# Longer leads for the steps behind GpSimd and for the steps that refill a stored weight buffer

## The chip, the cores and the metric

The kernel runs on one core of one Trainium2 chip. The metric is the device time of one execution in microseconds: the median of three runs before the change is 2082.1 us (2080.51 to 2083.09). Matrix products run on TensorE (PE in the profile), elementwise work on VectorE (DVE), ScalarE (ACT) and GpSimd (POOL), and all DMAs are issued by SyncE (SP).

## The reference

A hybrid decoder layer over 2048 tokens of width 1024. It applies an RMSNorm, one combined projection `h @ w_in`, eight heads of a gated delta rule, eight channel groups of a short gated convolution, an output projection with the residual, and a last RMSNorm:

```python
proj = rmsnorm(x, norm_in_w) @ w_in          # q,k,v | z | beta,g | B,C,h,z of the convolutions
qkv  = silu(causal_conv4(qkv));  q, k = l2norm(q) * 128**-0.5, l2norm(k)
o    = gated_delta_rule(q, k, v, g, beta)    # triangular solve per chunk, state carried over chunks
o    = rmsnorm(o, gdn_norm_w) * silu(z)
y    = B * (causal_conv3(C * h) + conv_b) * silu(z_c)
out  = rmsnorm(x + concat(o, y) @ w_out, final_norm_w)
```

## The kernel before, in words

**Tiling.** The tokens are worked in two halves of 1024. The columns of `w_in` are taken in 32 pairs of 128 columns: `kq`, `vz` (a head's key and query, value and gate) and `ca`, `cb` (the convolutions). A pair of one half is one call of `quad`: a seven-product scheme (Strassen's kind) over 512-token blocks, each product 12 matmuls of 128x512 in fp16 (high and low parts), so 84 matmuls a quad, into the banks `ps_d`. A quad takes two of six large buffers `t4` for its results (three where a `vacc` is wanted), and the convolutions hand these back.

**Weights.** In the first half every pair's weights are made on the chip. `fetcher` loads two raw tiles (`raw`, four buffers, so two pairs). `scales` squares them on ScalarE (`junk_sq`), sums them over partitions with one small matmul (`ps_t<-wss,ones_b`) and calls `pow2_below` (line 504) for a power-of-two scale: a maximum on VectorE, a power on GpSimd (`p<-p,nhalf_pow`), a mask on VectorE (`p<-p,expo`), a product. `prepare_hi` (line 735) makes the five high parts on ScalarE, in the order G1, G2, G7, G3, G4. `prepare_lo` (line 749) makes the low parts on VectorE and the sums and differences `st` that they need; one sum, `raw<-raw`, goes to GpSimd or VectorE, whichever is free earlier (`either`). Each of the five buffers exists once: it is written again when its products of the pair before are done and its copy has been stored to DRAM (`keep`, `wc<-g`). The second half reads these copies back (`gr<-wc`) and makes no weights.

**Heads.** For each head `gdn` (line 1102) loads decays (`E`), masks them on GpSimd (`affine_select`), takes eight exponentials on ScalarE, forms `NA` from key products, has `invert` run 31 pairs of small GpSimd steps (`nbt`, `nbx`), and then steps through eight chunks: matmul, `r` on VectorE, matmul, `u` on ScalarE, matmul, the state `S_all` on VectorE.

**Order.** Each engine works its own queue strictly in the order written. That order is made by a planner in the kernel: a `Clock` with costs for each operation advances a time for each engine, generators are the tasks, and `do` (line 340) holds a step back until the planner's time lets it in:

```python
lead = LEAD[e] if lead is None else lead      # 0.0 for ACT, DVE and POOL
t = clk.ready(e, a, k)                        # inputs written, buffer free, by the planner's clock
cur, q = now(), clk.t[e]                      # planner's PE time, the engine's own queue time
late = t > (cur if lead < 0 else max(cur, q)) + lead
if not late and q <= cur + back: break        # then the step is written
```

With lead 0 a step may be written as soon as its inputs are ready by the time that the engine's own queue reaches it; `back` is 1.2. With a negative lead it is written only when the planner's PE time is that much past the moment of readiness. What other tasks write meanwhile goes in front. Some steps have negative leads already: the squares in `scales` (`SAFE`, -5.0) and some steps of the heads (`LATE`, -5.0; -3.0). `keep_order` then fixes each engine's order. The output projection follows at the end, with its own splitting (`split_mix`, which calls `pow2_below` 16 times).

All operations are written by one helper, so every row of the profile has its line, L204; tiles tell them apart.

Of the kernel before, what the change touches and what calls it, by code (L numbers as in the profile page):

```python
# [14 lines left out]
AF = mybir.ActivationFunctionType  # L15
ALU = mybir.AluOpType
# [8 lines left out]
PLAN = ((3, 2, 2, 2, 2, 2, 2, 1), (2, 1, 2, 1, 2, 1, 2, 0))  # L25
SAFE = -5.0
LATE = -5.0
LEAD = {"PE": -0.4, "ACT": 0.0, "DVE": 0.0, "POOL": 0.0, "SP": -2.0}
ORDER = ("PE", "ACT", "DVE", "POOL", "SP")

# [198 lines left out]
def hybrid_layer_kernel(ctx, tc, x, norm_in_w, w_in, conv_qkv_w, A_log, dt_bias, gdn_norm_w,  # L229
# [3 lines left out]
    PE, ACT, DVE, POOL, SP = (Engine(clk, r, k) for r, k in zip(  # L233
        (nc.tensor, nc.scalar, nc.vector, nc.gpsimd, nc.sync), ORDER))
# [52 lines left out]
    def now():  # L287
        return clk.t["PE"]

    def spawn(gen, prio=2):  # L290
        seq[0] += 1
        tasks.append([prio, seq[0], 0.0, gen])
        tasks.sort(key=lambda t: (t[0], t[1]))

    def mark(*key):
        done.add(key)
        marks[0] += 1
# [35 lines left out]
    def need(*keys):  # L333
        while not all(k in done for k in keys):
            yield None
# [4 lines left out]
    def do(fn, *a, back=BACK, lead=None, **k):  # L340
        e = fn.eng
        lead = LEAD[e] if lead is None else lead
        while True:
            t = clk.ready(e, a, k)
            cur, q = now(), clk.t[e]
            late = t > (cur if lead < 0 else max(cur, q)) + lead
            if not late and q <= cur + back:
                break
            yield max(t - max(lead, 0.0) if late else 0.0, q - back, cur + 0.1)
        fn(*a, **k)  # L350
# [21 lines left out]
    def rel(x, n=1):  # L372
        if isinstance(x, str):
            cred[x] += n
        else:
            name = x.tensor.name
            kind, tag = where.pop(name)
            where[tag] = clk.last.get(name, 0.0)
            slots[kind].append(tag)
        marks[0] += 1  # L380
# [13 lines left out]
    def either(n=512):  # L394
        return POOL if max(now(), clk.t["POOL"]) + 0.2 + 0.0026 * n <= \
            max(now(), clk.t["DVE"]) + 1.0 + 0.001 * n else DVE
# [107 lines left out]
    def pow2_below(o, sq, gain):  # L504
        n = sq.shape[-1]
        r = sm.tile([P, 2], F32, tag="p2", name="p2")[:, 0:n]
        yield from do(DVE.tensor_scalar, r, sq, 1e-30, None, op0=ALU.max)
        yield from do(POOL.tensor_tensor, r, r, nhalf_pow[:, 0:n], op=ALU.pow)
        yield from do(DVE.tensor_tensor, r.bitcast(I32), r.bitcast(I32), expo[:, 0:n].bitcast(I32),
                      op=ALU.bitwise_and)  # L510
        yield from do(DVE.tensor_scalar, o, r, gain, None, op0=ALU.mult)

    cols_x = const([P, KD], "cols_x")
# [10 lines left out]
    def scale_x():  # L524
        m = sm.tile([P, KD], F32, tag="m8", name="m8", bufs=1)
        yield from do(DVE.tensor_tensor, m, cols_b[:, 0:KD], cols_b[:, 0:KD], op=ALU.mult)
        m1 = sm.tile([P, 1], F32, tag="m1", name="m1", bufs=1)
        yield from do(DVE.tensor_reduce, m1, m, axis=AX.X, op=ALU.max)
        pt = yield from acq("t")
        yield from do(PE.transpose, pt[0:1, 0:P], m1, ident)  # L530
        m2 = sm.tile([1, 1], F32, tag="m2", name="m2", bufs=1)
        yield from do(DVE.tensor_reduce, m2, pt[0:1, 0:P], axis=AX.X, op=ALU.max)
        yield from do(PE.matmul, pt[:, P:P + 1], ones[0:1, :], m2, start=True, stop=True)
        yield from pow2_below(sx, pt[:, P:P + 1], 256.0)
        rel(pt)
        yield from do(DVE.reciprocal, isx, sx)
        yield from do(DVE.tensor_scalar, cols_x, cols_b[:, 0:KD], sx, None, op0=ALU.mult)
# [168 lines left out]
    def hold(kind):  # L706
        while cred[kind] == 0:
            yield None
        cred[kind] -= 1
# [21 lines left out]
    def parts_of(p):  # L731
        r1, r2 = raws[p, 0], raws[p, 1]
        return r1[:, 0:KT], r1[:, KT:KD], r2[:, 0:KT], r2[:, KT:KD]

    def prepare_hi():
        for p in range(NP):
            yield from need(("s", p))
            s1, s2 = wsc[:, p, 0:1], wsc[:, p, 1:2]
            for tag, dep, nk in (("G1", "s", KD), ("G2", "st", KT), ("G7", "st", KT), ("G3", "st", KD), ("G4", "a12", KT)):
                yield from need((dep, p))  # L740
                yield from hold(tag)
                g = wst.tile([P, 2, nk, P], F16, tag=tag, name="g", bufs=1)
                src = {"G1": lambda: raws[p, 0], "G2": lambda: held[p][:, 0], "G7": lambda: held[p][:, 1],
                       "G3": lambda: raws[p, 1], "G4": lambda: parts_of(p)[1]}[tag]()
                yield from do(ACT.activation, g[:, 0], src, AF.Copy, scale=s2 if tag == "G3" else s1)
                held[p, tag] = g, src
                mark("h", p, tag)

    def prepare_lo():
        def keep(g, at, p):  # L750
            n = 1
            for d in g.shape[1:]:
                n *= d
            yield from do(SP.dma_start, wcd[p][:, at * WG:at * WG + n], g.rearrange("p s k c -> p (s k c)"))

        def low(p, tag, js, at):
            yield from need(("h", p, tag))
            g, src = held.pop((p, tag))
            s = wsc[:, p, 1:2] if tag == "G3" else wsc[:, p, 0:1]
            yield from do(DVE.scalar_tensor_tensor, g[:, 1], src, s, g[:, 0], op0=ALU.mult, op1=ALU.subtract)  # L760
            for o, j in enumerate(js):
                ops[p, j] = lambda k, s, o=o: g[:, s, o * KT + k, :]
                mark("w", p, j)
            spawn(keep(g, at, p), 2)

        for p in range(NP):
            yield from need(("s", p))
            rho = wsc[:, p, 4:5]
            A11, A12, A21, A22 = parts_of(p)
            st = wst.tile([P, 2, KT, P], F32, tag="st", name="st")  # L770
            held[p] = st
            yield from low(p, "G1", (0, 1), 0)
            yield from do(DVE.scalar_tensor_tensor, st[:, 1], A21, rho, A11, op0=ALU.mult, op1=ALU.subtract)
            yield from do(either().tensor_tensor, A21, A21, A22, op=ALU.add)
            yield from do(DVE.scalar_tensor_tensor, st[:, 0], A21, rho, A11, op0=ALU.mult, op1=ALU.subtract)
            mark("st", p)
            yield from do(either().tensor_tensor, A12, A12, st[:, 0], op=ALU.subtract)
            mark("a12", p)
            yield from low(p, "G2", (2,), 2)
            yield from low(p, "G7", (3,), 3)  # L780
            yield from low(p, "G3", (4, 5), 4)
            rel("raw")
            yield from low(p, "G4", (6,), 6)
            rel("raw")
            del raws[p, 0], raws[p, 1], held[p]
        mark("prepared")
# [315 lines left out]
    def gdn(half, h, st):  # L1102
# [6 lines left out]
        beta, dec, ngc, gd = gts[half]  # L1109
        E = hd.tile([P, NC, P], F32, tag="E", name="E", bufs=2)  # L1110
# [1 line left out]
        yield from do(POOL.affine_select, out=E, in_=E, pattern=[[0, NC], [1, P]], compare_op=ALU.is_ge,  # L1112
                      fill=-1e30, base=0, channel_multiplier=-1)
        for c in range(NC):
            yield from do(ACT.activation, E[:, c, :], E[:, c, :], AF.Exp, bias=ngc[:, h, c:c + 1])
        yield from need(("kqt", half, h, 0))
        kqs = st["kq"]
        kss = sm.tile([P, NC], F32, tag="kss", name="kss")
# [24 lines left out]
        for b in range(2):  # L1143
# [8 lines left out]
            for i in range(CB):  # L1152
                c = b * CB + i
# [10 lines left out]
            for c0 in range(b * CB, b * CB + CB, 2):  # L1164
                pq = yield from acq("t")
                for i in range(2):
                    c = c0 + i
# [29 lines left out]
        for b in range(2):  # L1197
            yield from do(DVE.tensor_tensor, kqs[b][:, :, 1, :], qe[:, b * CB:(b + 1) * CB], kqs[b][:, :, 1, :],
                          op=ALU.mult, lead=LATE)

# [5 lines left out]
        for b in range(2):  # L1206
            sl = slice(b * CB, (b + 1) * CB)
            pv = yield from acq("t")
            for i in range(CB):
                c = b * CB + i  # L1210
# [8 lines left out]
        for a, q0 in ((0, 0), (2, 0), (1, 32)):  # L1219
            r0 = a * 32  # L1220
            yield from do(DVE.transpose, V[r0:r0 + 32, :, q0:q0 + 32], W[r0:r0 + 32, :, r0:r0 + 32],
                          lead=-3.0)
# [41 lines left out]
        for b in range(2):  # L1264
            po = yield from acq("o")
            po = po.rearrange("p (c i) -> p c i", i=P)
            for i in range(CB):
                c = b * CB + i
# [6 lines left out]
                else:  # L1275
                    yield from do(PE.matmul, pa, kq(c)[:, 0, :], S, start=True, stop=True)
                    yield from do(DVE.scalar_tensor_tensor, r, pa, dec[:, 0, h, c:c + 1], vp[:, c, :],
                                  op0=ALU.mult, op1=ALU.subtract, back=9.0)
# [7 lines left out]
                else:  # L1286
                    yield from do(DVE.scalar_tensor_tensor, S, S, dec[:, 2, h, c:c + 1], pe,
                                  op0=ALU.mult, op1=ALU.add, back=9.0)
# [5 lines left out]
    def gdn_post(half, h, b, po, qss):  # L1294
# [14 lines left out]
        yield from do(ACT.activation, osq, ocv, AF.Square)  # L1309
        yield from do(DVE.transpose, on, osq, lead=LATE)  # L1310
        op = sm.tile([P, nq], F32, tag="op", name="op")
# [12 lines left out]
        yield from do(DVE.tensor_tensor, ocv, ocv, osq, op=ALU.mult)  # L1324
        yield from do(DVE.scalar_tensor_tensor, zb, oc, gnw, zb, op0=ALU.mult, op1=ALU.mult, lead=LATE)
        t0 = half * NC + b * CB
# [202 lines left out]
    first_x()  # L1529
    spawn(scales(), 0)  # L1530
    spawn(prepare_hi(), 1)
    spawn(prepare_lo(), 1)
    spawn(gate_weights(), 1)
    spawn(use_rows(), 1)
# [8 lines left out]
    for n, (kind, half, i, p) in enumerate(plan):  # L1543
# [9 lines left out]
        if kind == "kq":  # L1553
            st = sts[half, i] = {}
# [83 lines left out]
```

## Time and profile before

| | |
|---|---|
| median of three runs | 2082.1 us |
| profiled execution | 2081.03 us, of it the span 2079.3 us |
| PE busy | 1918.4 us (92%) |
| VectorE busy | 1325.5 us (64%) |
| ScalarE busy | 964.2 us (46%) |
| GpSimd busy | 765.9 us (37%) |
| mean granted TensorE clock | 0.959 of full speed |
| DMA | 308.97 MB, mean 149 GB/s |

How to read it: the page gives an average over stages with different limits. The first 104 us load and normalise the tokens; up to about 950 us the first half makes its weights and multiplies; up to about 1740 us the second half multiplies with weights that are read back; then comes the output projection. The granted clock says at which share of its full speed TensorE was let run; its two levels are 1.2 and 2.4 GHz, so 0.5 and 1.0, and a value between is a stretch that held both. A wait in brackets behind a row is idle time of that engine before the instruction and the work that ended it.

### The profile page before, as it was taken

How to read it: one execution, taken by the hardware profiler on the slowest of the kernel's cores; microseconds unless marked ns; L12 is line 12 of the kernel's file. 1: busy time of each engine (PE TensorE's matmuls, PEld its weight loads, DVE VectorE, ACT ScalarE, POOL GpSimd, SP SyncE). 2: the span in 40 equal slices, each digit the busy share in tenths (PEclk: the TensorE clock that was granted, in tenths of full speed). 3: DMA queues.
4: the chain of work that ended last, by engine and by line, in shares of the span. 5: the costliest groups of instructions: out<-in, count | busy, mean ns of one | idle time of the engine just before them, and what ended most of it. 6: DMA issues, size and time to landing. Idle time of an engine off the chain costs nothing.

```text
span 2079.3 us, 30141 instructions
## 1 busy us (share of the span) xinstructions
PE 1918.4 (92%) x10832; PEld 1051.1 (51%) x10832; DVE 1325.5 (64%) x2559; ACT 964.2 (46%) x1871; POOL 765.9 (37%) x1330
## 2 busy tenths in 40 slices
PE   3798878898898898999999999999999998999998
PEld 2354444445454554455556556466565563444443
DVE  5897588788786877775657767756756543532311
ACT  6565556556564546453554544435334332532300
POOL 3226226372726373725154353551551511100000
PEclk9799879799998998999999999999999999999999
DMA  6368746666757765628464475654534438423110
GB/s 162 88 149 209 173 115 181 151 159 147 153 97 170 121 174 128 158 94 305 136 223 156 137 229 162 197 180 143 154 109 122 127 112 316 162 98 106 67 46 31
DMA packets 250140, 308.97 MB, mean 149 GB/s; under 512 B 66301, under 2 KB 179334, under 8 KB 249094
## 3 DMA queue, kind: packets, MB, share of 16 engines
q1 hardware_dynamic: 249990, 307.05, 53.1%
q8 instruction: 85, 1.39, 0.3%
q14 instruction: 65, 0.53, 0.1%
HBM read 194.65 MB, written 112.33 MB: 148 GB/s over the span
## 4 chain that ended last, share of the span: by engine, by line
PE 52%; DVE 3%; issue 1%; ACT 1%; DMA 1%; POOL 0%; SPq 0%; DVEq 0%; POOLq 0%; ACTq 0%
PE ps_d L204 43%; PE ps_t L204 5%; PE ps_r L204 3%; PE ps_o L204 2%; DVE kq L204 0%; DVE wo L204 0%; POOL oss L204 0%; DMA mr<-mixd 0%; DMA gr<-wc 0%; DVE c L204 0%; DVE ab L204 0%; ACT c L204 0%; DVE NA L204 0%; DVE vacc L204 0%; ACT junk_sq L204 0%
## 5 line engine op out<-in xcount | busy, mean ns | idle before, releaser
L204 PE MATMUL ps_d<-xop,g 128*128 128x512 f16 x2688 | 658.9, 393 | 31.0 <-ACT g L204 9.5
L204 PE MATMUL ps_d<-xop,gr 128*128 128x512 f16 x2688 | 643.6, 379 | 0.0
L204 PEld LDWEIGHTS <-g 128*128 128x128 f16 x2688 | 266.2, 101 | 335.5 <-issue 71.3
L204 PEld LDWEIGHTS <-gr 128*128 128x128 f16 x2688 | 261.0, 99 | 240.2 <-issue 0.4
L204 PE MATMUL ps_d<-wo,mm 128*128 128x512 f16 x1536 | 334.5, 381 | 6.6 <-ACT mm L204 6.2
L204 ACT ACTIVATE c<-ps_d 128x512 f32<-128x512 f32 x320 | 189.6, 592 | 324.9 <-PE ps_d L204 320.0
L204 POOL TENSOR_TENSOR nbt<-nbx,nb 128x60 f32<-128x60 f32 (+24 forms) x496 | 200.8, 405 | 121.3 <-DMA nb<-nd 84.7
L204 PEld LDWEIGHTS <-mm 128*128 128x128 f16 x1536 | 149.6, 98 | 189.3 <-ACT mm L204 8.0
L204 POOL TENSOR_TENSOR nbx<-nbx,nbt 128x60 f32<-128x60 f32 (+24 forms) x496 | 203.1, 409 | 38.1
L204 POOL TENSOR_TENSOR oss<-oss,nhalf_pow 128x16 f32<-128x16 f32 x32 | 100.1, 3127 | 160.5 <-DVE oss L204 159.8
L204 DVE SCALAR_TENSOR_TENSOR kq<-c,wq,kq 128x512 f32<-128x512 f32 x192 | 155.4, 812 | 4.3 <-ACT kq L204 0.3
L204 ACT ACTIVATE g<-raw,wsc 128x1024 f16<-128x1024 f32 (+1 forms) x96 | 95.4, 1000 | 76.5 <-PE ps_d L204 23.1
L204 DVE SCALAR_TENSOR_TENSOR res<-ps_d,msc,res 128x512 f32<-128x512 f32 x32 | 22.6, 747 | 168.8 <-PE ps_d L204 168.3
L204 POOL TENSOR_TENSOR p<-p,nhalf_pow 128x2 f32<-128x2 f32 (+1 forms) x51 | 41.1, 807 | 238.0 <-DVE p L204 219.9
L204 DVE SCALAR_TENSOR_TENSOR g<-raw,wsc,g 128x1024 f16<-128x1024 f32 (+1 forms) x96 | 108.2, 1134 | 27.1 <-ACT g L204 26.3
L204 DVE TENSOR_TENSOR c<-ps_d,c 128x512 f32<-128x512 f32 x128 | 87.6, 685 | 45.8 <-PE ps_d L204 43.3
L204 ACT ACTIVATE mm<-mr,msc 128x1024 f16<-128x1024 f32 x32 | 36.1, 1145 | 165.4 <-PE ps_d L204 125.1
L204 POOL TENSOR_TENSOR c<-c,c 128x512 f32<-128x512 f32 (+1 forms) x31 | 52.3, 1689 | 155.4 <-ACT c L204 100.4
L204 DVE TENSOR_TENSOR c<-c,c 128x512 f32<-128x512 f32 (+1 forms) x65 | 58.5, 900 | 72.4 <-ACT c L204 72.0
L204 POOL TENSOR_TENSOR stat<-stat,nhalf_pow 128x1 f32<-128x1 f32 x16 | 9.1, 566 | 233.3 <-DVE stat L204 233.3
L204 POOL TENSOR_TENSOR raw<-raw 128x512 f32<-128x512 f32 x32 | 45.4, 1418 | 132.8 <-DVE st L204 93.7
L204 ACT ACTIVATE u<-ps_r 128x128 f32<-128x128 f32 x128 | 35.0, 274 | 119.3 <-PE ps_r L204 118.4
(225 smaller groups left out, 2771.3 us busy)
## 6 DMA issues: line engine op xcount, KB each, us to landing
gr<-wc SPq DMA_DIRECT2D x96, 512.0 KB, 4.0
raw<-in_w_in_dram SPq DMA_DIRECT2D x64, 512.0 KB, 11.1
wc<-g SPq DMA_DIRECT2D x64, 512.0 KB, 9.1
wc<-g SPq DMA_DIRECT2D x96, 256.0 KB, 4.6
wor<-in_w_out_dram SPq DMA_DIRECT2D x32, 512.0 KB, 5.5
mr<-mixd SPq DMA_DIRECT2D x32, 512.0 KB, 5.1
x<-in_x_dram SPq DMA_DIRECT2D x16, 512.0 KB, 7.2
E<-gd SPq DMA_DIRECT2D x16, 512.0 KB, 6.8
```

Of the source, the lines that this page charges most:

```text
L204: return raw(*a, **k)
```

## The change

Four steps are written with a longer negative lead, by two new constants, `GP` (-1.2) and `ST` (-3.0):

- the mask behind GpSimd's power in `pow2_below` (VectorE, lead -1.2), in each of its calls;
- the second `st` of a pair, behind the sum that GpSimd may have made (VectorE, -1.2, from the second pair on);
- the five high parts of a pair on ScalarE (-3.0, from the third pair on);
- the eight exponentials of a head behind GpSimd's mask (ScalarE, -2.4).

No operation, buffer, DMA or wait is added or taken away.

```diff
+GP = -1.2
+ST = -3.0
 LEAD = {"PE": -0.4, "ACT": 0.0, "DVE": 0.0, "POOL": 0.0, "SP": -2.0}
...
         yield from do(POOL.tensor_tensor, r, r, nhalf_pow[:, 0:n], op=ALU.pow)
         yield from do(DVE.tensor_tensor, r.bitcast(I32), r.bitcast(I32), expo[:, 0:n].bitcast(I32),
-                      op=ALU.bitwise_and)
+                      op=ALU.bitwise_and, lead=GP)
...
-                yield from do(ACT.activation, g[:, 0], src, AF.Copy, scale=s2 if tag == "G3" else s1)
+                yield from do(ACT.activation, g[:, 0], src, AF.Copy, scale=s2 if tag == "G3" else s1,
+                              lead=ST if p > 1 else None)
...
             yield from do(either().tensor_tensor, A21, A21, A22, op=ALU.add)
-            yield from do(DVE.scalar_tensor_tensor, st[:, 0], A21, rho, A11, op0=ALU.mult, op1=ALU.subtract)
+            yield from do(DVE.scalar_tensor_tensor, st[:, 0], A21, rho, A11, op0=ALU.mult, op1=ALU.subtract, lead=GP if p else None)
...
-            yield from do(ACT.activation, E[:, c, :], E[:, c, :], AF.Exp, bias=ngc[:, h, c:c + 1])
+            yield from do(ACT.activation, E[:, c, :], E[:, c, :], AF.Exp, bias=ngc[:, h, c:c + 1], lead=2 * GP)
```

## Rows read from the trace of the kernel before

**Rows 1.** Busy time by stage: stretch, PE, PEld, DVE, ACT, POOL, clock, DMA share, GB/s.

```profile
0.00:104.00 104.00, 59.55 (x234) 29.34 (x235) 71.83 (x147) 63.44 (x109) 29.07 (x43) 0.84 0.50 125
104.00:950.00 846.00, 749.31 (x4209) 414.08 (x4208) 655.89 (x1253) 480.33 (x915) 400.57 (x609) 0.92 0.64 152
950.00:2079.30 1129.30, 1109.57 (x6392) 607.64 (x6390) 597.76 (x1161) 420.45 (x848) 336.28 (x678) 1.00 0.46 148
```

**Rows 2.** Waits, 104 to 950 us: who waited for whom, us, times, longest.

```profile
ACT g L204 <- DVE st L204: 34.2, 17, 4.1
...
DVE p L204 <- POOL p L204: 22.9, 9, 6.2
...
ACT g L204 <- PE ps_d L204: 21.7, 15, 2.9
DVE st L204 <- POOL raw L204: 20.5, 11, 3.8
...
ACT g L204 <- DMA wc<-g: 18.2, 5, 8.3
...
ACT g L204 <- DVE wsc L204: 14.8, 9, 3.9
...
ACT E L204 <- POOL E L204: 11.3, 5, 4.8
...
PE ps_d L204 <- ACT g L204: 8.2, 2, 5.4
```

**Rows 3.** Chain that ended last, its earliest step of work: start, us, what.

```profile
884.55 0.17 DVE p L204
```

**Rows 4.** Instructions in order of time, 878 to 887 us: start, us, instruction, [idle before].

```profile
884.55 0.16 DVE L204 TENSOR_TENSOR p<-p,expo 128x2 int32<-128x2 int32 x1 [6.21 <-POOL p L204]
...
885.94 0.60 PE L204 MATMUL ps_r<-r,Wt 128*128 128x128 f32 x2 [5.16 <-DVE r L204]
```

**Rows 5.** Instructions in order of time, 553 to 565 us.

```profile
562.47 0.72 ACT L204 ACTIVATE g<-raw,wsc 128x512 f16<-128x512 f32 x1 [8.90 <-POOL nbt L204]
...
564.29 0.79 PE L204 MATMUL ps_r<-r,Wt 128*128 128x128 f32 x2 [5.89 <-DVE r L204]
```

**Rows 6.** Instructions in order of time, 643 to 658 us.

```profile
652.75 0.72 ACT L204 ACTIVATE g<-raw,wsc 128x512 f16<-128x512 f32 x1 [8.35 <-DMA wc<-g]
...
657.26 0.16 PE L204 MATMUL ps_t<-wss,ones_b 128*128 128x2 bf16 x1 [9.79 <-ACT junk_sq L204]
```

**Rows 7.** Instructions in order of time, 239 to 246 us.

```profile
239.25 2.35 POOL L204 TENSOR_TENSOR c<-c,c 128x1024 f32<-128x1024 f32 x1
239.32 2.83 DVE L204 SCALAR_TENSOR_TENSOR st<-raw,wsc 128x512 f32<-128x512 f32 x1 [1.16 <-POOL raw L204]
...
242.18 1.33 ACT L204 ACTIVATE g<-st,wsc 128x512 f16<-128x512 f32 x2 [2.87 <-DVE st L204]
...
244.19 1.76 PE L204 MATMUL ps_t<-Wt,Q 64*64 64x64 f32 x16 [1.87 <-ACT Q L204]
```

**Rows 8.** PE's instructions, 768 to 774 us.

```profile
773.62 0.49 PE L204 MATMUL ps_o<-kq,S_all 128*128 128x128 f32 x2 [1.47 <-ACT oc L204]
```

**Rows 9.** Busy time in stretches of low clock (columns as in Rows 1).

```profile
473.00:483.00 10.00, 7.64 (x27) 5.57 (x28) 8.52 (x15) 8.93 (x21) 4.31 (x3) 0.51 0.66 132
...
655.00:665.00 10.00, 7.74 (x31) 3.54 (x31) 9.86 (x19) 5.84 (x10) 4.92 (x8) 0.71 0.91 258
...
sum 35.00, PE 27.90 PEld 16.09 DVE 26.58 ACT 25.08 POOL 14.66; mean PE 5.58 PEld 3.22 DVE 5.32 ACT 5.02 POOL 2.93
```

**Rows 10.** PE's instructions, 203 to 212 us.

```profile
210.33 1.04 PE L204 MATMUL ps_d<-xop,g 128*128 128x512 f16 x2 [5.41 <-ACT g L204]
```

**Rows 11.** Instructions in order of time, 270 to 290 us.

```profile
278.18 0.71 ACT L204 ACTIVATE g<-raw,wsc 128x512 f16<-128x512 f32 x1
...
288.47 1.91 PE L204 MATMUL ps_d<-xop,g 128*128 128x512 f16 x4
```

**Rows 12.** Groups of the trace by line and form: xcount, busy us, mean ns, idle before.

```profile
L204 DVE SCALAR_TENSOR_TENSOR st<-raw,wsc 128x512 f32<-128x512 f32 x64 | 50.7, 792 | 21.6 <-POOL raw L204 21.6
```

## The prediction

> **What bounds the kernel now.** I read the busy times by stage first. The reader is to see that only the first half has anything to give: from 104 to 950 us TensorE is busy 749.3 of 846 us, so 96.7 us idle, at a granted clock of 0.92, while from 950 us on it is busy 1109.6 of 1129.3 us at 1.00 [rows 1]. VectorE is busy 655.9 of those 846 us and ScalarE 480.3: neither is full, yet TensorE waits for both.
>
> Then the waits of that stage. The four steps that the change moves are waits at the head of a strictly ordered queue: on VectorE 22.9 us for GpSimd's power and 20.5 us for GpSimd's sum, on ScalarE 34.2, 21.7, 18.2 and 14.8 us before a high part `g`, and 11.3 us before the exponentials [rows 2]. That is 144 us of held queues. What counts is only what TensorE feels of it. The chain that ended last begins with just such a step, the mask of `pow2_below` [rows 3]; seen in order of time it had waited 6.21 us for GpSimd, and the recurrence step `r`, queued behind it on VectorE, then let TensorE wait 5.16 us [rows 4].
>
> I went through the stage in order of time and kept each wait of TensorE over 0.8 us whose releaser stood in a queue behind one of the four steps. There are ten, 32.5 us in all. Three are long: the one above, 5.89 us behind a `g` that waited 8.90 us [rows 5], and 9.79 us behind a `g` that waited 8.35 us for its buffer's store [rows 6]; 20.8 us together. Seven are short, 11.7 us together: the first is 1.87 us for a `Q` that stood behind a `g` on ScalarE [rows 7], the last 1.47 us for an `oc` [rows 8]. Five of the seven hang on ScalarE's queue (8.5 us), two on VectorE's (3.2 us). The other 64 us of TensorE's idle time have releasers that no moved step holds, or the weights themselves.
>
> Five stretches, 35 us, have a low clock right after such waits: TensorE is busy 27.9 us in them at a clock between 0.51 and 0.71 [rows 9].
>
> **The change, part by part.** No work is added or removed. A step with a lead of -L is written only once the planner's time is L past its readiness, so what others write in that time goes in front. Where the real wait is shorter than L it should vanish, where it is longer it should shrink by L. I take L itself, 1.2 for VectorE's and 3.0 (2.4 for the exponentials) for ScalarE's steps.
>
> *Short waits.* The five on ScalarE are below 3.0 and go whole: 8.5 us. Of the two on VectorE, behind the second `st`, I take half, 1.6, since a part of what comes forward is itself long. Together 10.1 (ends: 0 and 11.7).
>
> *Long waits.* They shrink by 3.0, 3.0 and 1.2: 7.2 us (ends: 0 and 20.8). The rest stays, because the lead is smaller than GpSimd's or the store's lateness: late next is the same step.
>
> *Clock.* At 0.61, the middle of the two rows, 27.9 us of busy time hold 27.9 x 0.39 = 10.9 us that full clock would save (8.1 to 13.7 by the ends). I take it in the share of the waits that go, 17.3 of 32.5: 5.8 us. Gross: 10.1 + 7.2 + 5.8 = 23.1 us.
>
> *What the pushed steps make late.* Along one pair the leads add up: 1.2 for the scale, 3.0 for G1, 1.2 for `st`, 3.0 for G2, so 8.4 us; G7, G3 and G4 follow on the same engine. Each high part carries its low part on VectorE, its store on SP's queue, and, behind G3 and G4, the load of the pair after next. This costs nothing where weights lie ready early. An early example: the last high part of a pair is written at 278.18 and its first product begins at 288.47 us, 10.3 us later, while TensorE works at the recurrence [rows 11]; 8.4 us more are hidden there. Where the weight is last, nothing hides it. TensorE waited 8.2 us in two places for ScalarE's `g` itself [rows 2], 5.41 of them at 210 us [rows 10]; these can't gain. Counting pairs in order of time, six of the 32 have a weight finished less than 4 us before its product begins (the fifth to eighth, the twelfth and the twenty-seventh). Below: 0, since each of these runs is followed by a stretch without products like that of rows 11, in which a delay is made up. Above: 6 x 8.4 = 50 us. I take two steps of 3.0, 6.0 us, near to the 8.2 that the rows show.
>
> *Start, second half, output.* The mask is moved at the start too (three calls, up to 1.2 us each, and TensorE is busy only 59.6 of 104 us there [rows 1]): 0, ends 0 and 3.6. In the second half and the output projection TensorE is full [rows 1], so the exponentials of the later heads and the 16 masks of the output stage move beside its work: 0; without that cover 1.2 us, once, where the first output tiles are split.
>
> Net: 23.1 - 6.0 = 17.1 us. From the profiled execution, 2081.0 us (span 2079.3 and 1.7 around it), that is 2063.9; the median of the runs is 1.1 us above it, so I forecast 2065 us.
>
> **A page that speaks against it.** While GpSimd summed from 239.25 to 241.60 us, VectorE's `st`, begun at 239.32, took 2.83 us [rows 7] where its mean is 0.79 [rows 12]: it ended 0.55 us after GpSimd did. So work that comes forward into a wait for GpSimd may itself be held by GpSimd. The Trainium skill, SBUF — State Buffer, section "Who interferes with whom", says that a VectorE instruction with two inputs in SBUF contends with a GpSimd instruction that reads SBUF, and that the one that issues second is blocked rather than slowed. By that rule, the trace agrees in this row; that it would hold most of the work brought forward no run here shows.
>
> **The rivals.**
>
> *The weights become the bound (slower).* If the six close pairs pay their 8.4 us and nothing is made up, 50 us are added and 23 won: 2082 + 27 = 2109 us. It decides from 23 us of unhidden delay, about three of the six pairs. For it: in the first half two raw tiles of the pair after next hang on G3 and G4, so a delay in one pair comes back two pairs later. Against it: the stretch of rows 11, and that each wait that the lead only replaces costs nothing new, which holds for the 14.8 us behind the scale and the 34.2 us behind `st` [rows 2].
>
> *Another wait takes the place of the long ones (little gain).* What comes forward on ScalarE is often work that waits for TensorE, so the three long waits stay; 10.1 us and a third of the clock, 3.4, less the 6.0: 7.5 us, 2075 us. For it: the 21.7 us that `g` waits for TensorE's own products are no lateness of GpSimd [rows 2]. Against it: the long waits have a recurrence step or the next squares right behind them, which were wanted [rows 4 to 6].
>
> *VectorE's brought-forward work is held by GpSimd.* The gain of VectorE's steps (1.6 and 1.2) is lost: ScalarE's 14.5 us and 4.9 of clock stay, 19.4. Some 20 waits for GpSimd on VectorE (9 and 11 in that stage) each hold a step 2.0 us longer (2.83 less 0.79), 40 us of queue, of which TensorE feels as much as now, 32.5 of 144 us: 9 us. With the 6.0 of late weights 4.4 us remain: 2078 us.
>
> *It doesn't do what it says.* If the real lateness lies so far from the planner's time that the order around these steps hardly improves, or a new order costs as much as it gives, the time stays at 2082 us. For it: lateness of 6 to 9 us against leads of 1.2 to 3.0 [rows 4 to 6].
>
> **How the numbers follow.** A measurement of this kernel can tell about 0.2% (4 us) from no change. Chances: forecast 0.42, weights the bound 0.25, little gain 0.16, held VectorE 0.07, nothing 0.10. Faster holds the forecast, the little gain and a third of the held case: 0.60. Same holds the rest of the held case and the case of nothing: 0.15. Slower 0.25. The forecast's own range is 2050 to 2077. For 8 in 10, the lower end allows most of the ten waits and of the clock to go (32.5 + 10.9 less 6.0 is 37, 2045); the upper goes into the slower case up to three quarters of its way (0.75 x 50 less 23 is 15 over, 2097).
>
> **What would show it.** Right: in 104 to 950 us of the new profile TensorE idle some 80 us instead of 97, `g`, `p`, `st` and `E` at the head of a queue well under half of their 144 us, no low clock after the short ones, the stage some 17 us shorter, and all later stages the same. Wrong: TensorE's waits for `g` itself well over 8.2 us, or stretches without products longer than now before a quad begins; then the weights have become the bound. If the held queues shrink and TensorE's idle time does not, the waits were hidden anyway.

## The result and the profile after

The changed kernel is slower: 2113.2 us (2112.0 to 2117.2, three runs) against 2082.1, a ratio of 1.0166 with the interval 1.0149 to 1.0182. The forecast was 2065 us, the range ended at 2097. What came is nearest to the slower rival, "the weights become the bound", priced at 2109. The profiled execution has a span of 2111.5 us for 2079.3, 32.2 more.

The waits that the change was to shorten did become shorter, all but those of the mask (22.9 us in nine waits before, 22.2 in nine after). Waits of VectorE and then of ScalarE from 104 to 950 us in the kernel after (who waited for whom: us, times, longest), against [rows 2]:

```profile
DVE p L206 <- POOL p L206: 22.2, 9, 4.8
...
DVE st L206 <- POOL raw L206: 9.5, 6, 5.0
...
ACT g L206 <- DMA wc<-g: 10.8, 3, 7.4
...
ACT g L206 <- DVE wsc L206: 5.7, 4, 2.9
...
ACT E L206 <- POOL E L206: 1.0, 1, 1.0
...
ACT g L206 <- DVE st L206: 0.3, 1, 0.3
```

The 143.6 us of held queues in [rows 2] (leaving out its last row, which is TensorE's) are 49.5 here: `g` behind `st` fell from 34.2 to 0.3 us, and its 21.7 us behind TensorE's products are gone. But ScalarE did not idle less for it: 365.7 us of these 846 before and 372.6 after. Another step stands at the head of its queue now, `c`, which copies a result of TensorE's products. Its wait rose by 62.4 us; before, then after:

```profile
ACT c L204 <- PE ps_d L204: 107.4, 81, 3.9
...
ACT c L206 <- PE ps_d L206: 169.8, 99, 8.0
```

And the stage is longer, since TensorE now waits for the weights. TensorE's waits, 104 to 950 us, in the kernel before:

```profile
PE ps_r L204 <- DVE r L204: 18.2, 9, 5.9
PE ps_t L204 <- ACT junk_sq L204: 16.7, 3, 9.8
...
PE ps_d L204 <- DVE g L204: 3.4, 4, 1.5
```

and in the kernel after:

```profile
PE ps_d L206 <- ACT g L206: 49.9, 15, 9.4
PE ps_d L206 <- DVE g L206: 32.9, 21, 4.0
...
PE ps_r L206 <- DVE r L206: 2.3, 3, 1.3
...
PE ps_t L206 <- ACT junk_sq L206: 0.4, 1, 0.4
```

The waits that the forecast meant to remove are nearly gone (`r` 18.2 to 2.3, `ps_t` behind `junk_sq` 16.7 to 0.4). The waits for high and low parts rose from 11.6 us in six places (8.2 in [rows 2] and the 3.4 above) to 82.8 us in 36.

Where a half ends shows in the group of the first half's products. The view of TensorE's instructions on tile `g` (count: shortest, median, longest ns, first and last start; then idle time before them by releaser, us and times, over the whole execution), before:

```profile
L204 PE MATMUL ps_d<-xop,g x2688: 376/379/634, 31.4 to 953.9; 128*128 128x512 f16 x192
...
  ACT g L204: 9.5, 3
...
  DVE g L204: 3.4, 4
```

and after:

```profile
L206 PE MATMUL ps_d<-xop,g x2688: 376/379/634, 31.0 to 994.7; 128*128 128x512 f16 x192
...
  ACT g L206: 51.2, 16
  DVE g L206: 32.9, 21
```

The last first-half product starts 40.8 us later; from there to the end the kernel after needs 8.6 us less (1116.8 for 1125.4), because work of the heads was done in the longer first half (112 matmuls `ps_r<-r,Wt` before that point, where it was 104). Busy time by stretch (stretch, length, PE, PEld, DVE, ACT, POOL, clock, DMA share, GB/s), before to the end of its first half:

```profile
104.00:954.00 850.00, 753.31 (x4231) 416.53 (x4230) 657.30 (x1257) 481.76 (x917) 400.57 (x609) 0.92 0.64 153
```

and after, the stretches that answer to [rows 1] and then to the end of its first half:

```profile
104.00:950.00 846.00, 730.41 (x4056) 388.33 (x4055) 637.78 (x1212) 473.38 (x898) 391.34 (x602) 0.92 0.62 144
950.00:2079.30 1129.30, 1113.21 (x6433) 615.68 (x6433) 607.76 (x1184) 433.03 (x870) 352.03 (x686) 0.99 0.47 153
...
104.00:995.00 891.00, 770.75 (x4273) 415.13 (x4272) 665.59 (x1271) 488.09 (x930) 416.31 (x661) 0.92 0.62 148
```

TensorE's idle time in that first half went from 96.7 (850.00 less 753.31) to 120.3 us, 23.6 more. It is the sum of two large numbers: the waits for weights, 71.2 us more, and all its other waits, 84.9 us before and 37.0 after, 47.9 less (waits of 0.15 us and less are not in these sums). The other 9 us of the 32.2 are busy time: 1927.5 us in the whole execution for 1918.4, with as many matmuls, at a mean clock of 0.956 for 0.959.

What a late weight looks like: one pair, the twenty-eighth, in both kernels in order of time (start, us, instruction, idle before and releaser). Before:

```profile
806.40 0.74 DVE L204 SCALAR_TENSOR_TENSOR st<-raw,wsc 128x512 f32<-128x512 f32 x1
807.18 1.33 ACT L204 ACTIVATE g<-st,wsc 128x512 f16<-128x512 f32 x2 [1.84 <-DVE st L204]
...
828.92 0.59 PE L204 MATMUL ps_d<-xop,g 128*128 128x512 f16 x2
```

After:

```profile
848.22 0.74 DVE L206 SCALAR_TENSOR_TENSOR st<-raw,wsc 128x512 f32<-128x512 f32 x1
...
848.94 0.60 ACT L206 ACTIVATE c<-ps_d 128x512 f32<-128x512 f32 x1 [1.02 <-PE ps_d L206]
849.44 1.14 ACT L206 ACTIVATE c<-c,wsc 128x1024 f32<-128x1024 f32 x1
852.13 0.63 ACT L206 ACTIVATE kq<-kq 128x512 f32<-128x512 f32 x1 [1.56 <-DVE kq L206]
852.67 1.32 ACT L206 ACTIVATE g<-st,wsc 128x512 f16<-128x512 f32 x2
853.43 0.60 PE L206 MATMUL ps_d<-xop,g 128*128 128x512 f16 x2
853.73 2.35 POOL L206 TENSOR_TENSOR c<-c,c 128x1024 f32<-128x1024 f32 x1 [2.96 <-DVE c L206]
854.40 2.23 DVE L206 SCALAR_TENSOR_TENSOR g<-st,wsc,g 128x512 f16<-128x512 f32 x1
856.68 1.69 PE L206 MATMUL ps_d<-xop,g 128*128 128x512 f16 x7 [1.73 <-DVE g L206]
```

Before, ScalarE stood idle 1.84 us at the head of its queue and wrote G2 and G7 0.04 us after the `st` that they need; G2's first product began 21.7 us later. After, the same `st` ended at 848.96 and G2 began at 852.67: `c`, `c` and `kq` had been written in front of it, and `kq` itself waited 1.56 us for VectorE. The product began 0.76 us after G2, and its low part, on VectorE, then cost TensorE 1.73 us.

### The profile page after: what moved, and what is told of

It reads as the page before. It is cut to its first block, busy times and chain, and to the rows that moved or that the text cites. A ratio compares the mean times of both kernels' runs of the same rounds, so it can differ in the third digit from the quotient of the medians.

```text
span 2111.5 us, 30116 instructions
## 1 busy us (share of the span) xinstructions
PE 1927.5 (91%) x10832; PEld 1044.0 (49%) x10832; DVE 1319.1 (62%) x2547; ACT 969.4 (46%) x1879; POOL 775.2 (37%) x1334
## 4 chain that ended last, share of the span: by engine, by line
PE 60%; DVE 6%; POOL 5%; DMA 4%; issue 3%; ACT 1%; SPq 1%; DVEq 0%; POOLq 0%; ACTq 0%
PE ps_d L206 49%; PE ps_t L206 6%; PE ps_r L206 3%; DMA wc<-g 2%; POOL nbx L206 2%; POOL nbt L206 2%; PE ps_o L206 2%; DMA raw<-in_w_in_dram 1%; DVE g L206 1%; DVE kq L206 1%; SPq L206 1%; DVE c L206 1%; DVE vacc L206 1%; ACT junk_sq L206 0%; POOL oss L206 0%
## 5 line engine op out<-in xcount | busy, mean ns | idle before, releaser
L206 PE MATMUL ps_d<-xop,g 128*128 128x512 f16 x2688 | 684.3, 401 | 102.5 <-ACT g L206 51.2
L206 POOL TENSOR_TENSOR c<-c,c 128x512 f32<-128x512 f32 (+1 forms) x34 | 59.0, 1735 | 250.9 <-ACT c L206 171.0
L206 DVE TENSOR_TENSOR c<-c,c 128x512 f32<-128x512 f32 (+1 forms) x62 | 53.4, 862 | 74.7 <-ACT c L206 74.2
## 6 DMA issues: line engine op xcount, KB each, us to landing
raw<-in_w_in_dram SPq DMA_DIRECT2D x64, 512.0 KB, 11.3
```

The source lines that it names most:

```text
L206: return raw(*a, **k)
```

## The experiments

**Theory.** The weights are made in a loop: squares of a pair, mask, G1, `st`, G2 to G4, then the raw load of the pair after next, whose squares follow. Each lead lengthens every round of the loop, the delays add up over the rounds, and the weights fall behind TensorE. **Rivals.** One of the other steps does the harm (mask, `st`, exponentials); or the kernel after merely has an unlucky order, since any change of a lead makes the planner draw the whole order anew. The expectations call the loop Theory 1. In e1 to e5 Theory 2 is a loss of each step by its own place in the queue and Theory 3 the unlucky order, which is Theory 2 in r1 to r4.

Each run below is timed against the kernel before in the same batch (2080.1 to 2082.4 us). "Ends" is the start of the last first-half product, "weights" the sum of the two idle rows of that view, "loop" a twelfth of the time from the squares of the fifth pair to those of the twenty-ninth, read from four such rows as these, before:

```profile
145.44 1.05 ACT L204 ACTIVATE junk_sq<-raw 128x1024 bf16<-128x1024 f32 x1
...
803.01 1.06 ACT L204 ACTIVATE junk_sq<-raw 128x1024 bf16<-128x1024 f32 x1 [0.51 <-DMA raw<-in_w_in_dram]
```

and after:

```profile
151.94 1.04 ACT L206 ACTIVATE junk_sq<-raw 128x1024 bf16<-128x1024 f32 x1
...
845.35 1.06 ACT L206 ACTIVATE junk_sq<-raw 128x1024 bf16<-128x1024 f32 x1
```

so 54.8 us a round before and 57.8 after; 12 rounds of 3.0 us, and 6.5 us that the fifth pair was late already, are the 42.3 us by which the later squares start later. "Loop" is a pace and no cause by itself: a weight buffer is written again only when its products are done, so a slower TensorE makes the round longer too.

| run | us | ratio (95%) | ends | weights | loop |
|---|---|---|---|---|---|
| before | 2082.1 | | 953.9 | 12.9 | 54.8 |
| after | 2113.2 | 1.0166 (1.0149 to 1.0182) | 994.7 | 84.1 | 57.8 |
| e1 mask alone | 2058.0 | 0.9889 (0.9874 to 0.9904) | 936.3 | 23.5 | 54.9 |
| e2 second `st` alone | 2046.9 | 0.9842 (0.9822 to 0.9863) | 930.8 | 13.4 | 54.5 |
| e3 high parts alone | 2105.3 | 1.0120 (1.0093 to 1.0147) | 973.8 | 64.7 | 57.2 |
| e4 exponentials alone | 2070.1 | 0.9952 (0.9934 to 0.9971) | 948.0 | 13.5 | 55.8 |
| e5 all but the high parts | 2061.5 | 0.9912 (0.9888 to 0.9935) | 932.3 | 27.5 | 54.5 |
| e6 high parts, buffer only | 2072.5 | 0.9951 (0.9933 to 0.9970) | 938.3 | 39.3 | 55.1 |
| e7 after, squares early | 2110.4 | 1.0154 (1.0123 to 1.0184) | 987.1 | 47.1 | 57.3 |
| e8 before, squares late | 2101.1 | 1.0090 (1.0054 to 1.0125) | 981.2 | 48.3 | 57.4 |
| e9 lead on G1, G2 only | 2082.0 | 0.9989 (0.9975 to 1.0002) | 944.6 | 42.2 | 54.9 |
| e10 on G7, G3, G4 only | 2052.4 | 0.9847 (0.9832 to 0.9861) | 930.9 | 33.6 | 54.7 |
| e11 high parts at -1.5 | 2078.7 | 0.9980 (0.9970 to 0.9991) | 952.9 | 26.1 | 56.5 |
| e12 second `st` at -1.5 | 2077.8 | 0.9979 (0.9961 to 0.9998) | 958.8 | 14.7 | 55.7 |
| r1 after, `GP` -1.1 | 2105.4 | 1.0134 (1.0110 to 1.0158) | 982.4 | 55.4 | 57.3 |
| r2 after, `GP` -1.3 | 2112.4 | 1.0169 (1.0145 to 1.0193) | 985.3 | 45.1 | 57.7 |
| r3 before, `LATE` -4.9 | 2076.9 | 0.9996 (0.9980 to 1.0012) | 959.4 | 12.6 | 55.4 |
| r4 before, `LATE` -5.1 | 2074.8 | 0.9978 (0.9964 to 0.9991) | 943.5 | 14.7 | 56.0 |
| g1 second `st`, G7, G3, G4 | 2060.5 | 0.9909 (0.9876 to 0.9942) | 931.5 | 12.3 | 54.6 |
| g2 mask and second `st` | 2063.0 | 0.9921 (0.9900 to 0.9942) | 933.7 | 19.7 | 55.5 |

### Each part alone: e1 to e4

The kernel before with one of the four edits of the change each, and nothing else of it:

```diff
+                      op=ALU.bitwise_and, lead=GP)                               # e1
+            ... st[:, 0], A21, rho, A11, ..., lead=GP if p else None)            # e2
+                              lead=ST if p > 1 else None)                        # e3
+            ... AF.Exp, bias=ngc[:, h, c:c + 1], lead=2 * GP)                    # e4
```

> Only the mask behind GpSimd's power keeps its lead of -1.2; the other three steps are as before. Theory 1 (the weights' loop: load of two raw tiles, squares, scale, five high and low parts, load of the pair after next; its delays add up, and the slack of some 10 us before each quad is used up first): 1.2 of 8.4 us stay inside the slack, so 2075 to 2088 us. Theory 2 (each step loses by its own place in the queue, whatever the loop): a share of the 31 us by the number of moved steps, 32 of 192 on the path, 5 us, 2087 us. Theory 3 (any new order is as good as another, the loss is chance): anything between 2050 and 2115 us.

> Only the second st keeps its lead of -1.2. Theory 1: 1.2 us in the loop, inside the slack, 2075 to 2088 us. Theory 2: about 5 us, 2087 us. Theory 3: anything between 2050 and 2115 us.

> Only the five high parts keep their lead of -3.0. Theory 1: 6.0 us in the loop (G1 and G2), most of the slack of 10 us gone and a good part of the loss there: 2095 to 2110 us. Theory 2: the largest share by number, 25 us, 2107 us. Theory 3: anything between 2050 and 2115 us.

> Only the exponentials keep their lead of -2.4. Theory 1: they are not in the weights' loop, 2075 to 2085 us, and the first half's idle time of TensorE for g stays near 12 us. Theory 2: no share on the path, 2082 us. Theory 3: anything between 2050 and 2115 us.

Three parts make the kernel faster by 10 to 33 us; the high parts alone make it slower by 25, which fits both Theory 1 and Theory 2. The three gains fit neither: e1, e2 and e4 came 17, 28 and 5 us below the lower end of Theory 1, and Theory 2 expected 2082 to 2087 us. Theory 3's wide range holds e1 and e4, and e2 lies 3 us below it. The view of tile `g` for e3:

```profile
L206 PE MATMUL ps_d<-xop,g x2688: 376/379/634, 32.1 to 973.8; 128*128 128x512 f16 x192
...
  ACT g L206: 40.0, 12
  DVE g L206: 24.7, 17
```

That is the picture of the kernel after, from one edit of the four. The single effects don't add: they sum to 40 us faster where the whole is 31 slower.

### The change without its high parts, and with another condition: e5, e6

e5 is the change with the edit of e3 left out. e6 keeps a condition on the high parts, but counts the 3.0 us only from when the buffer is free, not from when the inputs are there:

```diff
-                              lead=ST if p > 1 else None)
+                              slot=ST if p > 1 else None)
...
+            if slot is not None and clk.free(e, a, k) > cur + slot:
+                late = True
```

> The whole change but the lead of the high parts: mask, second st and exponentials keep theirs. Theory 1 (the weights' loop): the loop grows by only 2.4 of 8.4 us and keeps its slack, so the gains of the three parts alone (22, 33 and 10 us) hold in part: 2020 to 2055 us, TensorE's waits for g in 104 to 950 us under 30 us. Theory 2 (each step loses by its own place): contradicted already by the three parts alone; no number. Theory 3 (any new order is as good as another): independent draws, 2045 to 2110 us.

> The whole change, but the high parts' lead of -3.0 counts only from the moment at which their buffer is free, not from the moment at which their inputs (scale, st) are written. Theory 1: where the loop is close the buffer has been free for long (the matmuls of the pair before ended 9 to 30 us ahead), so nothing is added to the loop: near the kernel without the lead of the high parts, within 10 us of it, and well below 2082 us. If instead the wait for the buffer were what the lead makes expensive, it stays near 2113 us. Theory 3: 2045 to 2110 us, with no relation to it.

e5 came a little above its expected 2020 to 2055 us, because the gains of e1, e2 and e4 don't add, but the sign turns: the lead on the high parts is worth 52 us of time lost in this company. e6 has the loop of before and is 41 us faster than the kernel after: waiting out a buffer that is not stored yet does no such harm. It stands 11 us above e5, just outside the 10 us expected; the redrawn orders below differ by up to 8 us, and e2 and e12 by 31.

### The loop lengthened or shortened by the squares: e7, e8

The same 8.4 us by another step of the loop. e8 delays the squares in the kernel before, and takes over nothing of the change; e7 gives 4 us back in the kernel after:

```diff
-SAFE = -5.0
+SAFE = -13.4      # e8, in the kernel before
+SAFE = -1.0       # e7, in the kernel after
```

> The changed kernel with the lead of the squares at -1.0 instead of -5.0: the same loop is shortened by 4.0 us at a place that the change does not touch, all four new leads stay. Theory 1: two thirds to all of the loss comes back, since 4.0 of 8.4 us in a loop that now has no slack are 16 loops x 4.0 = 64 us at most and the other limits of some 2045 to 2080 us stand behind it: 2070 to 2095 us. Theory 3 or a loss at the moved steps' own places: 2105 to 2120 us.

> The kernel before, none of the four leads, with the lead of the squares at -13.4 instead of -5.0: the loop gets the 8.4 us that the change adds, at a place where no queue of VectorE is involved. Theory 1: slower by 20 to 45 us, 2100 to 2125 us, with TensorE's waits for g well over 11.6 us in 104 to 950 us. Loss at the moved steps' own places: 2075 to 2090 us.

e8 is the most direct test of Theory 1 and came as expected: 19 us slower, with the loop of the kernel after. Its view of tile `g`:

```profile
L204 PE MATMUL ps_d<-xop,g x2688: 376/379/634, 32.3 to 981.2; 128*128 128x512 f16 x192
...
  ACT g L204: 26.0, 15
  DVE g L204: 22.3, 19
```

e7 missed: at 2110.4 us it did not become faster, as an unlucky order or a loss at the moved steps' own places would have it (2105 to 2120). Its ScalarE (waits, 104 to 995 us) shows what the edit did instead:

```profile
ACT junk_sq L206 <- DMA raw<-in_w_in_dram: 40.4, 7, 14.7
```

In the kernel after this row is 8.9 us, in one place. The squares now stood at the head of ScalarE's queue before their load had landed, so the loop stayed at 57.3 us and everything behind them waited. So e7 did not give the loop its 4 us back, and it neither supports nor refutes Theory 1. It shows one thing more: TensorE's waits for weights fell to 47.1 us from 84.1, and the time hardly moved.

### Which high parts, and how far: e9 to e11

The whole change, but the lead of 3.0 only for some of the five, or half of it for all:

```diff
+                              lead=ST if p > 1 and tag in ("G1", "G2") else None)         # e9
+                              lead=ST if p > 1 and tag in ("G7", "G3", "G4") else None)   # e10
+ST = -1.5                                                                               # e11
```

> The whole change, but the lead of -3.0 on G1 and G2 alone; G7, G3 and G4 as before. Theory 1 (delays add up along the weights' loop): G1 waits for the scale and G2 for st, so these two carry all 6.0 us: 2098 to 2118 us, mean time from the squares of a pair to those of the pair after next over 57 us. If it is the number of pushed steps that costs, two fifths of the 50 us that the lead adds to the kernel without it, 2080 us.

> The whole change, but the lead of -3.0 on G7, G3 and G4 alone. Theory 1: their inputs and buffers are ready when their turn comes, so the lead adds nothing to the loop: 2052 to 2072 us, near the kernel without the lead (2061), squares to squares under 56 us. If it is the number of pushed steps, three fifths of 50 us, 2091 us.

> The whole change with -1.5 instead of -3.0 for the high parts. Theory 1: 3.0 instead of 6.0 us more in the loop, of which the slack of some 5 us that is left with the other three leads takes more than half: 2062 to 2092 us, between the kernels without and with the lead (2061 and 2113). If the order is redrawn by chance, anywhere from 2045 to 2115 us.

e10 and e11 fell within their expectations. e9 missed, by 16 us: G1 and G2 carry the lead on the path that I had summed, waits for weights are nearly as long as in e8 (42.2 us for 48.3), and yet the loop is as short as before. The number of pushed steps gave 2080 us for e9, which is near, but 2091 for e10, which is 39 off. Against e5 the lead on G1 and G2 costs about 20 us, on G7, G3 and G4 it gains 9, on all five it costs 52. So in these orders it takes the two together, and neither the sum of leads along one path nor their number describes it.

### How much is the luck of an order: e12, r1 to r4

e12 is e2 with -1.5 for -1.2. r1 and r2 are the kernel after and r3 and r4 the kernel before, with a constant changed by 0.1, so that the order is drawn anew and the leads in the loop stay within 0.1 us of what they were:

```diff
+GP = -1.5      # e12, with the edit of e2
+GP = -1.1      # r1;  -1.3 in r2
+LATE = -4.9    # r3;  -5.1 in r4
```

> Only the second st, with -1.5 instead of -1.2: a small step beside the fastest kernel so far (2047), to see how far the time of one part moves by a new order alone. If the 33 us are the second st's own, 2040 to 2058 us; if part of them is a lucky order, 2058 to 2085 us.

> The whole change, with GP at -1.1 for -1.2: each of its steps keeps its place in the queue within 0.1 us (0.2 for the exponentials), but the planner's order is drawn anew. Theory 1 (the leads of the high parts lengthen the weights' loop): 2095 to 2120 us, and TensorE waits 30 us or more for high parts between 104 and 995 us. Theory 2 (the kernel after had an unlucky order): anywhere from 2045 to 2115, with about an even chance of less than 2082.

> The whole change, with GP at -1.3 for -1.2, again only to draw the order anew. Theory 1: 2095 to 2120 us, with waits for high parts of 30 us or more. Theory 2: anywhere from 2045 to 2115, and not on the same side as the kernel after more often than chance has it.

> The kernel before, with the common lead LATE at -4.9 for -5.0: no part of the change, the order drawn anew. Theory 1 (the loop as short as before): 2050 to 2090 us, waits for high parts below 25 us. Theory 2: anywhere from 2045 to 2115.

> The kernel before, with LATE at -5.1 for -5.0, the order drawn anew in the other direction. Theory 1: 2050 to 2090 us, waits for high parts below 25 us. Theory 2: anywhere from 2045 to 2115.

e12 is 31 us slower than e2, from 0.3 us in one lead: much of a single order's time is a draw. The four redrawn kernels show how wide the draw is near these two points: 2105.4 and 2112.4 around the kernel after, 2076.9 and 2074.8 around the kernel before. The groups (with the two kernels themselves, 2105 to 2113 and 2075 to 2082) don't overlap. Over all runs it is clearer still: the five kernels with the lead of 3.0 on all five high parts (after, e3, e7, r1, r2) take 2105 to 2113 us; all others but e8, which delays the squares, take 2047 to 2082 (fourteen, with e6, whose 3.0 us count from the buffer alone). An unlucky order alone does not give that. Views of tile `g`, r1 and r3:

```profile
L206 PE MATMUL ps_d<-xop,g x2688: 376/379/634, 31.6 to 982.4; 128*128 128x512 f16 x192
...
  ACT g L206: 28.8, 13
  DVE g L206: 26.6, 20
```

```profile
L204 PE MATMUL ps_d<-xop,g x2688: 376/379/634, 31.8 to 959.4; 128*128 128x512 f16 x192
...
  ACT g L204: 9.1, 3
  DVE g L204: 3.5, 4
```

The times of all four fall in Theory 1's ranges, but its sign fails in r1 and r2: TensorE waited 27.5 and 15.3 us for high parts from 104 us to the end of the first half, not 30 or more. In r2 (waits of TensorE, 104 to 985.8 us):

```profile
PE ps_d L206 <- DVE g L206: 28.5, 15, 4.0
...
PE ps_d L206 <- ACT g L206: 15.3, 8, 4.6
```

These 43.8 us are hardly more than the 41.0 of e9, which is 30 us faster. TensorE's idle time in the first half of r2 is as long as in the kernel after (120.9 us for 120.3), but 77 us of it are other waits, where the kernel after has 37; in e7 it is 66 beside 45.8 for weights. So the lead on all five high parts makes the kernel slow in each order drawn, but what TensorE waits for differs from order to order.

### Versions meant to beat both: g1, g2

What gained alone and left the loop short, two at a time: the second `st` with the lead on G7, G3 and G4 (g1), the mask with the second `st` (g2).

> Only the second st (-1.2) and the high parts G7, G3 and G4 (-3.0) with a lead. Theory 1 (what leaves the loop alone gains): 2035 to 2075 us, loop as before, waits for high parts below 33 us. If the single gains add up: 35 us of the second st and 9 of the three high parts, 2038 us. Rival (each gain is one order's luck, any lead on high parts costs): 2080 or more.

> Only the mask and the second st (-1.2 each) with a lead. If the single gains add up, 24 and 35 us below 2082: 2023 us. Theory 1 with orders that scatter by 12 to 15 us: 2045 to 2075. Rival (luck alone): anywhere from 2045 to 2115.

Both beat both kernels, by 20 and 18 us against before, and neither beats e2 or e10. The gains of e1 and e2 (22 and 33) don't add to 55. Eight kernels move steps behind GpSimd and put no lead on G1 and G2 (e1, e2, e4, e5, e10, e12, g1, g2): 2047 to 2078 us, mean 2061, where the kernel before and its two neighbours have 2075 to 2082. That such moves gain, on the mean, is what the runs show; which of them is best they don't, with single orders up to 17 us to either side.

## Why the prediction was wrong

**A gain of the forecast's size exists, but not from the steps it was forecast for.** The ten waits behind moved steps were to give 17.3 us and the clock 5.8. In e5, the change without its high parts, TensorE's waits other than for weights fell from 84.9 to 52.8 us, those for weights rose by 14.6, so that the idle time of the first half fell by 17.3; the granted clock of that half is 0.94 for 0.92, and the kernel came at 2061.5 us, near the 2065 of the forecast. That is luck. About 12 of the 17.3 us were to come from the high parts, which e5 leaves out: 6.0 from the two long waits behind a `g`, and 6.4 from four of the five short ones on ScalarE, which by the trace (waits that end at 244.19, 271.52, 462.69 and 773.62 us) stand behind a `g` too. The mask, the second `st` and the exponentials were to give the other 5, and alone they gave 22, 33 and 10 us. Why so much, the runs don't show; e12 puts much of the 33 down to one order. In the kernel after the other waits fell even further, by 47.9; part of that is no gain, since a TensorE that waits for weights comes later to what it would have waited for.

**The step that failed is "what the pushed steps make late".** I took 6.0 us for it, two steps of 3.0, with 50 us as the upper end. By time it cost 52 us: so much slower is the kernel after than e5, the same change without the lead on the high parts. TensorE's waits for weights rose by even more, 71.2 us, and stand in 36 places where it was six. The slower rival's 2109 us was near the 2113.2, but its 50 us were six pairs of 8.4 us; what came was a little in nearly every pair, so that number is near by luck as well. By the prediction's own count, over the pairs with the lead (from the third on), a weight is finished less than 4 us before its product begins in 28 of 30, where it was in seven (the six that it names, and the third with 3.2 us). Three parts of its working were wrong:

- *"Each of these runs is followed by a stretch without products like that of rows 11, in which a delay is made up."* I counted pairs one by one, by how early each weight lay ready in the trace of before ([rows 11]). But a pair's weights start when the weights of the pair two before are done, so the delay of a round is still there in the next. On average (third to last pair, from the instruction times) G1's low part was ready 10 us ahead of its first product. In the kernel after 2.7 us are left; from the fifth pair on only two pairs, the nineteenth and the twenty-first, have 10 us again, and G2's low part ends 0.6 us after the first product of G2 has begun, where it was 9.7 us ahead. The rival named this feedback, but its price of 50 us still counted six pairs.
- *"Each wait that the lead only replaces costs nothing new, which holds for the 14.8 us behind the scale and the 34.2 us behind `st`."* These waits went, to 5.7 and 0.3 us, and the high parts came later for it. Over the fifth to the twenty-eighth pair the mean from the second `st`'s start to G2's start rose from 1.57 to 4.10 us, from the mask to G1 from 2.29 to 3.69. In the pair shown above, the high part that waited at the head of the queue left 0.04 us after its `st`; behind `c`, `c` and `kq` it also waited for what they wait for. In e5 and e10 27.2 and 21.1 us of `g` behind `st` remain, and they are among the faster kernels.
- *The sum of 8.4 us a pair.* Of the 5.9 us that the four places along a pair took in the mean (squares to mask 1.2, mask to G1 1.4, G1 to `st` 0.7, `st` to G2 2.5) the rest of the loop gave back 3.4, and the round grew by 2.5 us in this mean (3.0 between the two squares rows above). The 30 pairs with the lead make 15 rounds in twos, 37 to 45 us, and the first half ended 40.8 later. What was wrong is less the size of a step than the number of rounds that pay it. But a round pays only what the rest of the loop can't give back: in e9 the same four places took 4.7 us more than before, the rest gave all of it back, and the round was no longer.

**The clock did not come.** TensorE's granted clock in the first half stayed at 0.92: TensorE was idle 23.6 us more, not 17 us less.

**Of the signs I had named one told the truth.** "TensorE's waits for `g` itself well over 8.2 us" was the sign of the rival, and stood at 49.9. "At the head of a queue well under half of their 144 us" was named as a sign of success, and was met with 49.5 us in the slower kernel: it is no sign of success, since `c` took the place of `g` at the head of ScalarE's queue.

**What stays open.** Why G1 and G2 alone leave the loop short (e9) while all five lengthen it; why r2 and e7 are as slow as the kernel after with about half of its waits for weights; and how the 52 us between e5 and the kernel after divide between the loop and the luck of those two orders. That the lead on all five high parts costs the time is shown; that it does so through the loop is supported by e8 and by the weights' lost reserve, and not settled. No run tests whether the longer waits of `c` at the head of ScalarE's queue are a cause of the slow round or only follow from it.

## What to carry to other kernels

Before a step of a prefetch loop (one that makes or loads the operands of later rounds) is pushed back, sum its delay over the rounds and not over the instances that look close now: ask what its end starts, and whether that comes back to the same step. An idle wait at the head of a queue may be what keeps a loop short; judge it by who stands behind it, by who waits for the step itself, and by what would take its place at the head. Where a planner draws the order, time several neighbours of each version before a difference of one or two per cent is put down to an edit.

## What the runs showed of the hardware

The chain that ended last begins at 884.55 us in the kernel before [rows 3]. In the kernel after it reaches back 430 us further, into the first half. Its earliest piece is again a scale of the weights, and its two longest pieces before the end of the first half are transfers of their loop (start, us, what):

```profile
452.63 0.68 POOL p L206
...
571.28 21.80 DMA wc<-g
667.27 23.46 DMA raw<-in_w_in_dram
```

The page of the profile gives 4.5 us (256 KB) and 9.4 us (512 KB) from issue to landing as the medians of such stores and 11.3 of such loads, all issued by SyncE. That single ones take more than twice as long I had not reckoned with; in the kernel after, with 2.7 us of reserve left, they stand in the chain that ended last.

GpSimd held VectorE again, as in [rows 7]. In the pair shown above the low part of G2, begun at 854.40 while GpSimd added 128x1024, took 2.23 us, where the median of such low parts is 0.75; it ended 0.55 us after GpSimd did, the same 0.55 as there, and TensorE waited 1.73 us for it. Not every GpSimd instruction does this: the low part begun at 357.69 us of the kernel after, while GpSimd took a power (`oss`, 128x16, 3.46 us by the profile), took 0.75 us and ended 1.43 us before the power did.
